# Every second k step of the projections with its two products in reverse order

## The chip, the cores and the metric

The kernel runs on one core of one Trainium2 chip. The metric is the device time of one execution in microseconds (us). PE is the matrix engine, ACT the scalar engine, DVE the vector engine, POOL GpSimd and SP the engine that issues most of the transfers.

## The reference

One layer of a streaming encoder over 256 tokens of width 2048, all in fp32:

```python
u = rms_norm(h, norm_mix[l])
proj = u @ w_in[l]
o_dn = gated_deltanet(...)       # 8 heads, chunked delta rule
o_mla = mla_attention(...)       # 8 heads, latent attention
h = h + jnp.concatenate([o_dn, o_mla], axis=-1) @ w_out[l]
h = h + memory_cross_attention(rms_norm(h, norm_xattn[l]), mem_n, xa_wq, xa_wk, xa_wv, xa_wo)
h = h + conv_ffn(rms_norm(h, norm_ffn[l]), ffn_w_up, ffn_conv, ffn_conv_bias, ffn_w_down)
return rms_norm(h, norm_final)
```

Most of the work is in the weight matrices: 2048 x 4944 in, 2048 x 2048 out, four of 2048 x 2048 in the cross-attention, 2048 x 11264 up and 5632 x 2048 down.

## The kernel before

**A product.** Tokens lie in the free dimension, features on the 128 partitions. A number of 32 bits is kept as the sum of two parts in the fp32r type, high (`wh`, `xh`) and low (`wl`, `xl`), and a product is the sum of three: high by high, high by low, low by high. An input tile for one k chunk of 128 features is 128 x 512: 256 tokens' high parts and beside them their low parts. So `kstep` (lines 112 to 114) needs two matmuls for a k chunk: `wh` by all 512 columns (line 113), then `wl` by the first 256 (line 114). Both add into the same PSUM tile `ps` of 512 columns; its two halves are summed when the tile is evacuated. Each matmul brings a load of its own 128 x 128 block of weights.

**The groups.** A block of 128 output features takes one `ps` and 16 k steps (`gemm_block`), 8 for the two parts of the output projection and 44 for the down projection. The weights come in tiles of 128 x 1024, which are 8 k steps. For each tile SP issues a transfer of 512 KB into `raw`, ACT casts it to `wh` (line 102), DVE subtracts to get `wl` (line 103). `raw`, `wh` and `wl` have four buffers each. While the heads are computed these two run in two pieces of 512 columns.

**Who uses what.** `kstep` runs in the input projection (moving tile `u`), both parts of the output projection (`om`, `od`), the keys' and the output projection of the cross-attention (`mh`, `xo`), the up projection (`fx`) and the down projection (`ga`, `gb`) but its last block. Two other forms stand for comparison. `kstep3` (lines 117 to 119) has three matmuls of 256 columns, all into the first half of `ps`: in the latents' projections (`lath`), in the cross-attention's query projection (`xq`), scores (`kh`) and mixing (`pTx`), and in the last block of the down projection (`ga`, `gb`). The values' projection `v_block` (lines 950 to 952) streams weights past stationary tokens, three matmuls of 512 columns.

**What sets the order.** PE's order is the program's own, written out by hand. While the heads of the two attention groups are worked out, k steps of the input projection and of the output projection's first part are drawn one by one from a queue (`drawn`, `fill`, `until`) wherever PE would wait for the other engines; the constants at lines 20 to 22 say how many. The order on ACT, DVE and POOL is set by a scheduler that works with its own estimate of the durations.

Of the kernel before, what the change touches and what calls it, by code (L numbers as in the profile page):

```python
# [15 lines left out]
PSUM = bass.MemoryType.PSUM  # L16
# k steps drawn from the queue of products where the tensor engine would wait for other engines
F_BEFORE_MLA, F_BEFORE_DN1 = 8, 20                # in blocks
F_MLA, F_LEVEL, F_PRE, F_SOLVE = (6, 2, 4, 9), (3, 4, 5), (21, 6), 45
F_SCAN, F_NORM, F_SQ = 5, 28, 42  # L20

P = 128
T = 256            # tokens, and memory tokens
D = 2048
KC = D // P        # 16 chunks of the model width
DFF = 5632
NF = DFF // P      # 44 chunks of the hidden width
NH = 8             # heads of DeltaNet and of the latent attention
EPS = 1e-6
NEG = -1e30  # L30
B0 = 16            # blocks inverted by substitution, then doubled
LEVELS = (16,)
# a block's entries by column: first and last column, first row
COLS = ((0, 4, 1), (4, 8, 5), (8, 12, 9), (12, 15, 13))
NB = sum((j1 - j0) * (B0 - r0) for j0, j1, r0 in COLS)

# columns of the packed per-partition parameters
_c = 0
# [17 lines left out]

# columns of the constants, which depend on shapes alone
_c = 0
# [12 lines left out]
def trunk(ctx, tc, a):  # L71
    nc = tc.nc
    V, S, PE = nc.vector, nc.scalar, nc.tensor
# [20 lines left out]

# [1 line left out]
    def split_w(raw, n, pieces=1):  # L96
# [13 lines left out]

    # one k step: weights stationary, tokens moving; the two halves of ps are summed later
    def kstep(ps, wh, wl, xh2, first, last):
        PE.matmul(ps[:, 0:512], wh, xh2, start=first, stop=last, skip_group_check=True)  # L113
        PE.matmul(ps[:, 0:256], wl, xh2[:, 0:256], start=False, stop=last, skip_group_check=True)  # L114

# [34 lines left out]

# [1 line left out]
    cg = const.tile([P, NCG], F32, name="cg")  # L152
# [5 lines left out]

    # reciprocal norms as columns, and spread out as rows
    def rstd_col(*accs):  # L160
# [17 lines left out]

    # =================== phase 1: the two head groups ===================
    u = hl_tile("u")  # L180
    ctx.enter_context(tc.manual_schedule(engines={mybir.EngineType.PE}))
    with ExitStack() as ph:
# [11 lines left out]
        with tc.tile_pool(name="xpool", bufs=1) as xpl:  # L194
            xt = xpl.tile([P, KC, T], F32, name="xt")
            nc.sync.dma_start(sm[:, 0:KC], a["sm"][:, 0:KC])
            raw0 = wpool.tile([P, 1024], F32, name="raw", tag="raw")
            for c in range(4):
                nc.sync.dma_start(raw0[:, c * 256:(c + 1) * 256], a["w_in"][0][:, c * 256:(c + 1) * 256])
                nc.sync.dma_start(xt[:, 2 * c:2 * c + 2], a["x"][:, 2 * c:2 * c + 2, :])  # L200
            w0 = [split_w(raw0, 1024, 4)]
            nc.sync.dma_start(xt[:, 8:12], a["x"][:, 8:12, :])
            w0.append(load_w(a["w_in"][1], pieces=2))
            nc.sync.dma_start(xt[:, 12:16], a["x"][:, 12:16, :])
            for k in range(KC):
                split_gain(u(k), xt[:, k], sm[:, C_MIX + k:C_MIX + k + 1])
            ps0 = psg()
            for k in range(KC):
                wh, wl = w0[k // 8]
                j = k % 8  # L210
                kstep(ps0, wh[:, j * P:(j + 1) * P], wl[:, j * P:(j + 1) * P], u(k), k == 0, k == KC - 1)
            ps1 = gemm_block(a["w_in"], 1, u)
            lead = load_w(a["w_in"][4], pieces=2)
            nc.sync.dma_start(cg, a["cg"])
            nc.sync.dma_start(sm[:, KC:NSM], a["sm"][:, KC:NSM])
            nc.sync.dma_start(co, a["co"][:, 0:NCO])
            # sums of squares, half of them on GpSimd
            sqs = [p1.tile([P, 4, T], F32, name="xsq", tag="qkv2", bufs=2) for _ in range(2)]
            for k in range(KC):
                a2 = accs[k % 2]  # L220
                if k < 2:
                    S.activation(a2, xt[:, k], AF.Square)
                else:
                    sq = sqs[k // 4 % 2][:, k % 4]
                    S.activation(sq, xt[:, k], AF.Square)
                    (nc.gpsimd, V)[k % 2].tensor_add(a2, a2, sq)
            nc.sync.dma_start(posi, a["pos"].partition_broadcast(P))

        gbT = p1.tile([P, 2, P], F32, name="gbT")
        # cumulated log decay as columns  # L230
        gc = p1.tile([P, 2, NH], F32, name="gc")
        ngc = p1.tile([P, 2, NH], F32, name="ngc")
        nbe = p1.tile([P, NH], F32, name="nbe")
        # rows of beta and of the cumulated decay, spread over the partitions by way of DRAM
        rows = ph.enter_context(tc.tile_pool(name="rows", bufs=1, space=bass.MemoryType.DRAM))
# [9 lines left out]

# [1 line left out]
        cbuf = [p1.tile([P, T + 3], F32, name=f"cbuf{i}") for i in range(2)]  # L247
# [4 lines left out]

        # a queue of products, drawn on k step by k step where the tensor engine would wait
        queue = []
# [32 lines left out]
        pos, later = [0], []  # L287
        ahead = [2]
# [18 lines left out]
        def dn_qkv(g):  # L307
# [26 lines left out]
            def norms(sq, w, i):  # L334
                ps = psa("c")
                if w == 0:       # squared norms of the queries, as columns
                    for t in range(2):
# [4 lines left out]
                    return  # L342
                # keys of unit length
                n = sq[:, 2 * i:2 * i + 2]
# [9 lines left out]

        # the latents' blocks come first, and the first two are under way
        lats = []
# [6 lines left out]
        with ExitStack() as ms:  # L363
# [3 lines left out]
            nc.sync.dma_start(cm, a["co"][:, K_MLA:K_MLA + 384])  # L367
# [1 line left out]
            ql = mp.tile([P, 4, T], F32, name="ql", tag="kn")  # L369
# [23 lines left out]
            ps = psa()  # L393
# [11 lines left out]

# [1 line left out]
            ang = mp.tile([P, T], F32, name="ang", tag="m1k", bufs=4)  # L407
# [20 lines left out]
            fill(3)  # L428
# [1 line left out]
            kx2 = mp.tile([P, T], F32, name="kx2", tag="m1k", bufs=4)  # L430
# [35 lines left out]
            ps = psa()  # L466
# [5 lines left out]
            ps = psa()  # L472
# [10 lines left out]

# [1 line left out]
            until(Q0 + F_BEFORE_MLA * KC)  # L485

# [1 line left out]
            qpe = mp.tile([P, 4, T], F32, name="qpe")  # L488
# [20 lines left out]

            for i in range(2):           # rotary parts: all first halves, all second halves of 4 heads  # L510
                x1 = mp.tile([P, T], F32, name="qx1", tag="m1k", bufs=4)
# [51 lines left out]
            fill(F[2])  # L563
            for i in range(2):           # 4 heads at a time
                kn = mp.tile([P, 4, T], F32, name="kn", tag="kn")
# [37 lines left out]

# [1 line left out]
        dp = ph.enter_context(tc.tile_pool(name="dn", bufs=1))  # L605
# [10 lines left out]
        def delta(g):  # L616
# [26 lines left out]
            for t in range(2):  # L643
# [3 lines left out]
                V.tensor_mul(dd[t], per4(pm), et[t])  # L647
                # the diagonal blocks, side by side, and each row's turn
                tt[t] = dp.tile([P, 4, P], F32, name="tt", tag="tt", bufs=2)
# [18 lines left out]

            # every partition gets its block, and solves for its column of the block's inverse
            blk = dp.tile([P, 8, NB], F32, name="blk")  # L670
# [43 lines left out]

            # inverse of the unit lower triangular matrix, by doubling its diagonal blocks
            for li in range(len(LEVELS)):
# [20 lines left out]
                fill(F_LEVEL[2])  # L737
            # the last doublings, of which only the blocks under the diagonal are worked out
            for s in (32, 64):
# [33 lines left out]

            # first chunk, before which the state is zero, then the second; the outputs have tokens on partitions
            vn = [None, None]
# [37 lines left out]
            out_sq(po1, 1)  # L813
            # their norm (the query's enters through its epsilon), and back
            V.tensor_add(on, on, nq)
# [52 lines left out]

# [1 line left out]
        mhs = []  # L870
# [30 lines left out]

    # =================== output projection, residual ===================
    x2pool = ctx.enter_context(tc.tile_pool(name="x2pool", bufs=1))
# [158 lines left out]

    # =================== gated convolutional feed-forward ===================
    with ExitStack() as ph:
# [34 lines left out]

        # the square root's table, ahead of its use  # L1100
        warm = small.tile([P, 1], F32, name="warm")
# [26 lines left out]

# [1 line left out]
def _feat(v):  # L1130
# [110 lines left out]
```

## Time and profile before

| | |
|---|---|
| median of 3 runs | 1597.02 us |
| the runs | 1596.87 to 1598.11 us |
| the profiled execution, first to last instruction (its span; the profile lists no other time for it) | 1598.0 us |
| PE busy | 1565.8 us, 98% |
| DVE busy | 1115.5 us, 70% |
| ACT busy | 876.6 us, 55% |
| two lines of `kstep` in the chain that ended last | 71% |

The chain that ended last is the list of work, followed back from the last instruction, in which each piece was waited for by the next. PE's busy time counts a product from its start to its modelled end, and these overlap: with products one behind another PE is always busy, whatever the distance between their starts. So its pace is read from the starts in the timeline, or from the mean duration of a group, and not from the busy share.

### The profile page before, as it was taken

How to read it: one execution, taken by the hardware profiler on the slowest of the kernel's cores; microseconds unless marked ns; L12 is line 12 of the kernel's file. 1: busy time of each engine (PE TensorE's matmuls, PEld its weight loads, DVE VectorE, ACT ScalarE, POOL GpSimd, SP SyncE). 2: the span in 40 equal slices, each digit the busy share in tenths (PEclk: the TensorE clock that was granted, in tenths of full speed). 3: DMA queues.
4: the chain of work that ended last, by engine and by line, in shares of the span. 5: the costliest groups of instructions: out<-in, count | busy, mean ns of one | idle time of the engine just before them, and what ended most of it. 6: DMA issues, size and time to landing. Idle time of an engine off the chain costs nothing.

```text
span 1598.0 us, 24744 instructions
## 1 busy us (share of the span) xinstructions
PE 1565.8 (98%) x9386; PEld 1367.6 (86%) x9386; DVE 1115.5 (70%) x1810; ACT 876.6 (55%) x1474; POOL 145.2 (9%) x152
## 2 busy tenths in 40 slices
PE   7999999999999999999999999999999999999996
PEld 5887887888888889999888888888888888888886
DVE  7787688687975555666777777777787876445453
ACT  7767666847654444454556555555555555433341
POOL 2224011002310000000110000000000000111112
PEclk9999999999999999999999999999999999999998
DMA  7564444353655555544555555555555556665663
GB/s 251 173 204 143 144 134 136 126 199 120 215 194 186 188 190 189 178 137 146 179 189 180 188 188 184 185 185 186 187 188 189 186 184 178 185 191 177 194 182 107
DMA packets 80775, 282.25 MB, mean 177 GB/s; under 512 B 9392, under 2 KB 10304, under 8 KB 80656
## 3 DMA queue, kind: packets, MB, share of 16 engines
q1 hardware_dynamic: 79344, 277.86, 53.5%
q0 software_dynamic: 1312, 2.80, 0.6%
q8 instruction: 74, 1.21, 0.3%
q14 instruction: 45, 0.37, 0.1%
HBM read 277.83 MB, written 2.11 MB: 175 GB/s over the span
## 4 chain that ended last, share of the span: by engine, by line
PE 89%; DVE 6%; ACT 3%; issue 1%; DMA 1%; SPq 0%; DVEq 0%; ACTq 0%
PE psg L113 47%; PE psg L114 24%; PE psg L117 3%; PE psg L118 2%; PE psg L119 2%; DVE wl L103 2%; PE psg L952 2%; PE psg L950 2%; PE psg L951 2%; ACT wh L102 1%; DVE qkv L322 1%; DMA raw<-in_w_out_dram 1%; PE psa L612 0%; PE psa L531 0%; PE psa L530 0%
## 5 line engine op out<-in xcount | busy, mean ns | idle before, releaser
L103 DVE TENSOR_TENSOR wl<-raw,wh 128x1024 fp32r<-128x1024 f32 (+2 forms) x614 | 648.7, 1062 | 388.2 <-ACT wh L102 385.1
L102 ACT CAST wh<-raw 128x1024 fp32r<-128x1024 f32 (+2 forms) x614 | 551.5, 908 | 598.9 <-PE psg L113 373.7
L113 PE MATMUL psg<-fx,wh 128*128 128x512 f32 x1408 | 497.8, 397 | 0.0
L114 PE MATMUL psg<-fx,wl 128*128 128x256 f32 x1408 | 395.6, 281 | 0.0
L113 PEld LDWEIGHTS psg<-fx,wh 128*128 128x128 f32 x1408 | 264.7, 188 | 65.3
L114 PEld LDWEIGHTS psg<-fx,wl 128*128 128x128 f32 x1408 | 264.3, 188 | 0.0
L113 PE MATMUL psg<-u,wh 128*128 128x512 f32 x624 | 233.9, 413 | 9.0 <-DVE u L141 8.0
L114 PE MATMUL psg<-u,wl 128*128 128x256 f32 x624 | 177.5, 284 | 1.7 <-DVE wl L103 1.7
L113 PEld LDWEIGHTS psg<-u,wh 128*128 128x128 f32 x624 | 119.5, 191 | 39.6 <-DVE u L141 8.9
L113 PE MATMUL psg<-gb,wh 128*128 128x512 f32 x420 | 149.1, 397 | 0.0
L114 PEld LDWEIGHTS psg<-u,wl 128*128 128x128 f32 x624 | 119.6, 192 | 3.4 <-DVE wl L103 2.7
L114 PE MATMUL psg<-gb,wl 128*128 128x256 f32 x420 | 118.0, 281 | 0.0
L113 PEld LDWEIGHTS psg<-gb,wh 128*128 128x128 f32 x420 | 79.0, 188 | 19.5
L113 PE MATMUL psg<-mh,wh 128*128 128x512 f32 x256 | 90.7, 398 | 0.0
L113 PE MATMUL psg<-xo,wh 128*128 128x512 f32 x256 | 90.7, 398 | 0.0
L1081 DVE SCALAR_TENSOR_TENSOR y<-ub,sm,y 128x256 f32<-128x256 f32 x176 | 84.8, 482 | 3.1
L113 PE MATMUL psg<-ga,wh 128*128 128x512 f32 x240 | 85.5, 397 | 0.0
L114 PEld LDWEIGHTS psg<-gb,wl 128*128 128x128 f32 x420 | 78.8, 188 | 0.0
L114 PE MATMUL psg<-xo,wl 128*128 128x256 f32 x256 | 71.9, 281 | 0.0
L114 PE MATMUL psg<-mh,wl 128*128 128x256 f32 x256 | 71.9, 281 | 0.0
L117 PE MATMUL psg<-xq,wh 128*128 128x256 f32 x256 | 71.2, 278 | 0.0
L118 PE MATMUL psg<-xq,wh 128*128 128x256 f32 x256 | 70.9, 277 | 0.0
(405 smaller groups left out, 2487.2 us busy)
## 6 DMA issues: line engine op xcount, KB each, us to landing
raw<-in_w_up_dram SPq DMA_DIRECT2D x176, 512.0 KB, 3.5
raw<-in_w_down_dram SPq DMA_DIRECT2D x80, 512.0 KB, 4.1
raw<-in_w_in_dram SPq DMA_DIRECT2D x77, 512.0 KB, 3.8
raw<-in_w_out_dram SPq DMA_DIRECT2D x32, 512.0 KB, 3.6
raw<-in_xa_wk_dram SPq DMA_DIRECT2D x32, 512.0 KB, 3.5
raw<-in_xa_wv_dram SPq DMA_DIRECT2D x32, 512.0 KB, 3.5
raw<-in_xa_wq_dram SPq DMA_DIRECT2D x32, 512.0 KB, 3.5
raw<-in_xa_wo_dram SPq DMA_DIRECT2D x32, 512.0 KB, 3.5
```

The source lines that it names most:

```text
L102: S.copy(wh[:, c], raw[:, c])
L103: V.tensor_sub(wl[:, c], raw[:, c], wh[:, c].bitcast(F32))
L113: PE.matmul(ps[:, 0:512], wh, xh2, start=first, stop=last, skip_group_check=True)
L114: PE.matmul(ps[:, 0:256], wl, xh2[:, 0:256], start=False, stop=last, skip_group_check=True)
L117: PE.matmul(ps[:, 0:T], wh, xh2[:, 0:T], start=first, stop=False)
L118: PE.matmul(ps[:, 0:T], wh, xh2[:, T:2 * T], start=False, stop=False)
L119: PE.matmul(ps[:, 0:T], wl, xh2[:, 0:T], start=False, stop=last)
L322: V.scalar_tensor_tensor(t[:, i], cb[:, j:j + T], sm[:, ch + j:ch + j + 1], t[:, i], ALU.mult, ALU.add)
L950: PE.matmul(pss[t], xh, wh[:, wk], start=(k == 0), stop=False)
L951: PE.matmul(pss[t], xh, wl[:, wk], start=False, stop=False)
L952: PE.matmul(pss[t], xl, wh[:, wk], start=False, stop=(k == KC - 1))
L1081: V.scalar_tensor_tensor(y, b[:, j:j + T], sm[:, cw + j:cw + j + 1], y, ALU.mult, ALU.add)
```

## The change

`kstep` gets a flag that turns with every step. On the first step of a group the order is as before, high then low. On the next it is low, then high, and so on in turn. A group always begins with the high part, which clears `ps`. Groups, and the tiles of 8 steps and pieces of 4 in them, have an even number of steps, so it is always the odd step of a tile that is reversed. Nothing else changes in the program; comments are gone, which moves the line numbers: lines 113 and 114 of before are 122 and 120 of after, 102 and 103 stay, 132 becomes 140.

```diff
     def kstep(ps, wh, wl, xh2, first, last):
-        PE.matmul(ps[:, 0:512], wh, xh2, start=first, stop=last, skip_group_check=True)
-        PE.matmul(ps[:, 0:256], wl, xh2[:, 0:256], start=False, stop=last, skip_group_check=True)
+        rev = turn_[0] and not first
+        turn_[0] = not rev
+        for lo in ((True, False) if rev else (False, True)):
+            if lo:
+                PE.matmul(ps[:, 0:256], wl, xh2[:, 0:256], start=False, stop=last, skip_group_check=True)
+            else:
+                PE.matmul(ps[:, 0:512], wh, xh2, start=first, stop=last, skip_group_check=True)
```

On PE, the first tile of weights of the up projection before (`fx0` is the input's first half, numbers are buffers):

```order
L113 MATMUL psg_8569<-fx0_8477,wh_8572 128x512
L114 MATMUL psg_8569<-fx0_8477,wl_8573 128x256
L113 MATMUL psg_8569<-fx0_8477,wh_8572 128x512
L114 MATMUL psg_8569<-fx0_8477,wl_8573 128x256
L113 MATMUL psg_8569<-fx0_8477,wh_8572 128x512
L114 MATMUL psg_8569<-fx0_8477,wl_8573 128x256
```

and after:

```order
L122 MATMUL psg_8569<-fx0_8477,wh_8572 128x512
L120 MATMUL psg_8569<-fx0_8477,wl_8573 128x256 x2
L122 MATMUL psg_8569<-fx0_8477,wh_8572 128x512 x2
L120 MATMUL psg_8569<-fx0_8477,wl_8573 128x256 x2
L122 MATMUL psg_8569<-fx0_8477,wh_8572 128x512 x2
```

The products of one size now stand in twos; the number of each is the same.

On ACT, in the input projection near 50 us, where casts for the next k steps stand between the evacuations of finished blocks (`half`), before:

```order
L102 CAST wh_506<-raw_504 128x512 x2
L424 ACTIVATE cos_735<-ang_733 128x256
L425 ACTIVATE cos_735<-cos_735 128x256
L102 CAST wh_531<-raw_529 128x512
L132 COPY half_499<-psg_458 128x256
L102 CAST wh_531<-raw_529 128x512
L145 ACTIVATE kacc_304<-cl_300 128x256
```

and after:

```order
L102 CAST wh_506<-raw_504 128x512 x2
L432 ACTIVATE cos_735<-ang_733 128x256
L433 ACTIVATE cos_735<-cos_735 128x256
L140 COPY half_499<-psg_458 128x256
L102 CAST wh_531<-raw_529 128x512 x2
L153 ACTIVATE kacc_304<-cl_300 128x256
```

The evacuation has moved ahead of one cast of half a tile. The scheduler moved others in the same way, mostly before 470 us; SP's order is unchanged.

## Rows read from the trace of the kernel before

**Rows 1.** The page: span, busy time of PE, chain by line.

```profile
span 1598.0 us, 24744 instructions
PE 1565.8 (98%) x9386; PEld 1367.6 (86%) x9386; DVE 1115.5 (70%) x1810; ACT 876.6 (55%) x1474; POOL 145.2 (9%) x152
PE psg L113 47%; PE psg L114 24%; PE psg L117 3%; PE psg L118 2%; PE psg L119 2%; DVE wl L103 2%; PE psg L952 2%; PE psg L950 2%; PE psg L951 2%; ACT wh L102 1%; DVE qkv L322 1%; DMA raw<-in_w_out_dram 1%; PE psa L612 0%; PE psa L531 0%; PE psa L530 0%
```

**Rows 2.** Waits of PE: total us, times, longest.

```profile
PE psg L113 <- DVE u L141: 8.0, 3, 6.5
...
PE psg L114 <- DVE wl L103: 1.7, 3, 1.2
...
PE psg L113 <- ACT wh L102: 0.9, 1, 0.9
```

**Rows 3.** Timeline of PE, up projection: start us, length us, product.

```profile
1000.20 0.40 PE L113 MATMUL psg<-fx,wh 128*128 128x512 f32 x1
1000.44 0.28 PE L114 MATMUL psg<-fx,wl 128*128 128x256 f32 x1
1000.56 0.40 PE L113 MATMUL psg<-fx,wh 128*128 128x512 f32 x1
...
1001.26 0.40 PE L113 MATMUL psg<-fx,wh 128*128 128x512 f32 x1
```

**Rows 4.** Products by form, count, busy us, mean ns: up, query, values, down, mixing.

```profile
L113 PE MATMUL psg<-fx,wh 128*128 128x512 f32 x1408 | 497.8, 397 | 0.0
L114 PE MATMUL psg<-fx,wl 128*128 128x256 f32 x1408 | 395.6, 281 | 0.0
...
L117 PE MATMUL psg<-xq,wh 128*128 128x256 f32 x256 | 71.2, 278 | 0.0
...
L119 PE MATMUL psg<-xq,wl 128*128 128x256 f32 x256 | 70.9, 277 | 0.0
...
L952 PE MATMUL psg<-wh,mh 128*128 128x512 f32 x128 | 50.3, 393 | 0.0
L950 PE MATMUL psg<-wh,mh 128*128 128x512 f32 x128 | 50.2, 392 | 0.0
L951 PE MATMUL psg<-wl,mh 128*128 128x512 f32 x128 | 49.9, 390 | 0.0
...
L118 PE MATMUL psb<-pTx,vh 128*128 128x256 f32 x16 | 4.5, 283 | 0.0
...
L118 PE MATMUL psg<-ga,wh 128*128 128x256 f32 x16 | 4.5, 281 | 0.0
```

**Rows 5.** Timeline of PE, query projection, three products a step.

```profile
619.20 0.28 PE L117 MATMUL psg<-xq,wh 128*128 128x256 f32 x1
...
619.54 0.28 PE L117 MATMUL psg<-xq,wh 128*128 128x256 f32 x1
```

**Rows 6.** Timeline of PE, mixing in the cross-attention, three products a step.

```profile
709.02 0.28 PE L117 MATMUL psb<-pTx,vh 128*128 128x256 f32 x1
...
709.38 0.28 PE L117 MATMUL psb<-pTx,vh 128*128 128x256 f32 x1
```

**Rows 7.** Line 113 in two stretches: us, PE busy (count), clock, DMA.

```profile
0.00:407.00 407.00, 281.00 (x752) 0.99 0.50 164
407.00:1598.00 1191.00, 957.63 (x2708) 1.00 0.56 181
```

**Rows 8.** ACT's longest wait, then subtraction and cast by form.

```profile
ACT wh L102 <- PE psg L113: 373.7, 270, 3.5
...
L103 DVE TENSOR_TENSOR wl<-raw,wh 128x1024 fp32r<-128x1024 f32 x412 | 506.9, 1230 | 326.1 <-ACT wh L102 323.5
...
L102 ACT CAST wh<-raw 128x1024 fp32r<-128x1024 f32 x412 | 433.1, 1051 | 528.8 <-PE psg L113 350.0 <-issue 94.7 <-PE psg L952 50.8
```

**Rows 9.** Timeline of PE, input projection just behind a gap.

```profile
321.38 0.39 PE L113 MATMUL psg<-u,wh 128*128 128x512 f32 x1
...
322.07 0.39 PE L113 MATMUL psg<-u,wh 128*128 128x512 f32 x1
...
322.77 0.40 PE L113 MATMUL psg<-u,wh 128*128 128x512 f32 x1
```

More of the change, by code (lines that the diff above doesn't have):

```diff
@@ L109, in load_w @@
         return split_w(raw, n, pieces)
+    turn_ = [False]
     def kstep(ps, wh, wl, xh2, first, last):
-        PE.matmul(ps[:, 0:512], wh, xh2, start=first, stop=last, skip_group_check=True)
-        PE.matmul(ps[:, 0:256], wl, xh2[:, 0:256], start=False, stop=last, skip_group_check=True)
+        rev = turn_[0] and not first
[5 more added lines that the diff above has]
+                PE.matmul(ps[:, 0:512], wh, xh2, start=first, stop=last, skip_group_check=True)
     def kstep3(ps, wh, wl, xh2, first, last):
```

## The prediction

> **What bounds the kernel now.** I read the page first. The matrix engine is busy for 1565.8 of 1598.0 us, and of the chain that ended last 71% is the two lines that the change touches [rows 1]. Then the waits of PE: the longest group is 8.0 us, and waits for the weights (wl, wh) come to 2.6 us [rows 2]. So the time is not a wait that could be removed. It is the pace at which PE puts one product behind another, and the third view is of that pace.
>
> I call H a product of 512 columns (high part) and L one of 256 (low part). In the feed-forward stretch H starts at 1000.20, L at 1000.44, the next H at 1000.56 and, two k steps later, another at 1001.26 [rows 3]: 1.06 us for three k steps of 768 columns, 0.353 each, some 0.235 from H to L and 0.118 from L to H. Each product brings one weight load with it, before the change and after it. The table by form has means to the nanosecond: 397 for H and 281 for L [rows 4]; their sum of 678 is 325 more than the k step's 353, so a mean is about 162 more than the step to the next product. The difference of two such means is therefore a difference of pace.
>
> The same columns run at other paces elsewhere in this trace. The query projection of the cross-attention has only L products, three for a step of 768 columns: from 619.20 to 619.54, 0.340 a step [rows 5], with means of 278 and 277 [rows 4]. The last block of the down projection has the same three products at 281, and the mixing with the values needs 709.02 to 709.38, 0.360 a step [rows 4, 6]. The values' projection has only H products, and their means are 393, 390 and 392, not 397 [rows 4]. So a product's pace depends on its neighbours or on the phase in which it meets them, by several per cent, with no wait shown. That is what this change can move.
>
> **The change part by part.** There are 752 k steps before 407 us and 2708 after it, 3460 in all [rows 7], which is 1730 pairs. First step of a pair: H L as before. Second step: L H. Nothing is added: matmuls, loads, columns and transfers stay as many, and the high part still opens each group. The pattern H L H L becomes H L L H: of the four steps from product to product, two (H to L, L to H) stay, and the other H to L and L to H become one L to L and one H to H.
>
> H term. In the values' projection an H between two H takes (393 + 390 + 392) / 3 = 391.7, against 397: 5.3 ns less [rows 4]. In the new order each H has one H and one L neighbour, so I count half, 2.65, twice a pair: 5.3 ns. The bounds are 0 and all of it, 10.6.
>
> L term. An L between two L takes 277 to 278 in the query projection, 281 in the last block of the down projection, 283 in the mixing, against 281: from 3.7 less to 2 more [rows 4]. Half of it, twice a pair, is between 3.7 less and 2 more. The last block comes straight out of the H L pattern, and there L is no faster than in it; the query projection has far more products (256 for each of its three lines). I take the middle of those two, 1.9 less.
>
> That is 7.2 ns a pair. After 407 us PE hardly waits: (2708 / 2) x 7.2 = 9.7 us. Before 407 us the steps fill gaps between the small products of the heads, in short runs, and less filling makes some waits longer; I count half: 376 x 3.6 = 1.4 us. Together 11 us. The profiled span is 1598.0, which is 1.0 above the median of the runs and within their spread, so I take the sum off the median: 1597 - 11 = 1586.
>
> What is moved besides:
> - The high part of a weight tile is now read last, not last but one, so its buffer comes free one L later, 0.118 us, and the cast that refills it (ACT line 102, which waits for PE's line 113 in 270 cases, 373.7 us in sum [rows 8]) starts that much later. Behind it in ACT's order stand evacuations of finished products. Four buffers rotate, so the cast still runs about three tiles of 8 x 0.353 = 2.8 us ahead of its use; cast and subtraction need 1.05 and 1.23 us [rows 8]. Cost: none. Without that cover it would be 0.118 us a tile, some 430 tiles, 51 us. The low part's buffer comes free earlier, and the weight transfers on SP, whose order doesn't change, wait for the subtraction and so move by 0.12 us at most.
> - An odd step is never the first of a tile or of a cast piece, so no product asks for the low part before it did.
> - At the end of a block H now comes last and evacuation waits for it. Both products had to be done before, so this costs nothing beyond the pace.
> - The order of work on ACT, DVE and GpSimd shifts a little, mostly before 470 us: evacuations stand one cast earlier. A cast then waits for a block's end and one copy more. PE waited only 0.9 us for casts and 1.7 us for subtractions in the whole run [rows 2], and tiles are two ahead there. I count 0, with 3 us to either side.
>
> One rule speaks against any effect. The rows show 0.235 and 0.118 us for products of 512 and 256 columns, and other paces for the same columns [rows 3 to 6]. The Trainium skill (TensorE: Matmul & The Clock Gate, Step-by-step: what each phase is for) says that the engine reads the streamed operand and the weights through two independent ports, and that loading the next weights takes no read bandwidth from the running product. By that rule the order can't matter and the sum would be 0, which is the first rival below; the trace has not agreed with it so far, as the same L product stands at 277, 281 and 283 ns.
>
> **The rivals.**
> *No change.* Each load costs its product the same in this stream whatever stands next to it. For it: the two means hold over 1408 products each [rows 4], and behind a gap two steps take 0.69 (321.38 to 322.07) but the next two 0.70 again (322.07 to 322.77) [rows 9]. The stream is drawn to its slow pace, and the last block stayed in it with L products alone. Against it: H products run faster among themselves [rows 4]. Time: 1597, within 3.
>
> *The fast pace.* The new pattern settles where the query projection is, 0.340 a step [rows 5]. Then 3460 x 13.3 ns = 46 us, 1551; for half of that, 1574. For it: this pace exists with as many loads per product, and the means of 256 products of a line are near it [rows 4]. Against it: it is there with L products alone.
>
> *Slower: the pairs of short products.* Two L in a row must each have a weight load beside only 0.118 us of streaming, and before the change an H always followed. If L to L then runs as in the mixing, 0.120 [rows 6], and H gains nothing, a pair costs 2 x 1.7 = 3.3 ns more: 5.8 us, 1603. If all products go at that pace, 0.360 against 0.353 a step, it is 23 us, 1620. It decides from an L to L step over 0.118 plus what H to H gives back.
>
> **How the numbers follow.** Forecast, some of the interference goes, 4 to 20 us: 0.43. No change: 0.30. Fast pace, over 20 us: 0.14. Slower: 0.13. About 0.2%, 3 us, is what a measurement of this kernel can tell from no change. So faster 0.57, same 0.30, slower 0.13. The range reaches down to three quarters of the fast pace (1597 - 35 = 1562) and up to the short pairs' 1603; about 0.85 lies in it.
>
> **What would show it.** In the profile of the changed kernel the mean of the 512-column groups (fx, gb, ga) should be near 394 instead of 397 and that of the 256-column groups near 280. From the first H of a pair to the next pair's first H the timeline should show 0.70 us where it is 0.707 now. PE's waits should stay under 25 us. If the means stay at 397 and 281, the first rival holds; 388 and 276 are the fast pace; an L over 282 is the slow rival. A longer wait of PE for wl or wh would show that the cover of the casts was thinner than I think, and then the whole sum is wrong.

## The result, and the profile after

The changed kernel takes 1580.49 us (median of 4, 1578.94 to 1581.17), the kernel before in the same session 1596.94. The ratio is 0.989, with an interval of 0.9878 to 0.9902: 16.4 us faster, where 11 were forecast, inside the range of 1562 to 1603.

The profiled execution took 1580.7 us in all, 1.8 more than its span. If as much lies around the span of before, that execution of before was one of the slower ones (1599.8), and so the two spans differ by 19.1 us, more than the medians do.

The page of the changed kernel, to be read beside [rows 1]: span and busy time.

```profile
span 1578.9 us, 24577 instructions
PE 1546.1 (98%) x9386; PEld 1358.5 (86%) x9386; DVE 1119.3 (71%) x1810; ACT 889.3 (56%) x1473; POOL 147.9 (9%) x152
```

The matrix engine has as many products as before, 9386, and as large a share of the span. Its waits, as total us, times, longest:

```profile
PE psg L122 <- DVE u L149: 8.2, 3, 6.5
...
PE psg L120 <- DVE wl L103: 1.7, 3, 1.1
...
PE psg L122 <- ACT wh L102: 0.6, 1, 0.6
```

Against [rows 2] nothing has gone: 8.0 is 8.2, 1.7 is 1.7, 0.9 is 0.6. So the time was not taken from a wait. The timeline of PE in the up projection (a line may merge two products of one form; start, us) shows where it was taken:

```profile
1000.31 0.39 PE L120 MATMUL psg<-fx,wl 128*128 128x256 f32 x2
1000.54 0.62 PE L122 MATMUL psg<-fx,wh 128*128 128x512 f32 x2
1001.00 0.39 PE L120 MATMUL psg<-fx,wl 128*128 128x256 f32 x2
1001.23 0.62 PE L122 MATMUL psg<-fx,wh 128*128 128x512 f32 x2
```

From one pair of high products to the next, 1000.54 to 1001.23, two k steps take 0.69 us, where [rows 3] have 0.707. The table by form gives it to the nanosecond (count, busy us, mean ns):

```profile
L122 PE MATMUL psg<-fx,wh 128*128 128x512 f32 x1408 | 439.8, 393 | 0.0
L120 PE MATMUL psg<-fx,wl 128*128 128x256 f32 x1408 | 277.6, 279 | 0.0
...
L122 PE MATMUL psg<-gb,wh 128*128 128x512 f32 x420 | 133.4, 393 | 0.0
L120 PE MATMUL psg<-gb,wl 128*128 128x256 f32 x420 | 82.8, 278 | 0.0
```

Against 397 and 281 in [rows 4], the high product is 4 ns shorter and the low one 2 to 3: four products, some 13 ns a pair. The two stretches of [rows 7] say the same. The table of windows for line 122, with as many k steps in each stretch as before:

```profile
0.00:405.50 405.50, 249.43 (x752) 0.99 0.50 164
405.50:1578.90 1173.40, 846.50 (x2708) 1.00 0.57 184
```

The stretch behind the heads went from 1191.0 to 1173.4 us: 17.6 us for 1354 pairs, 13.0 ns each. The stretch of the heads went from 407.0 to 405.5: 1.5 us for 376 pairs. The windows are cut at half microseconds; by the last product of the first output projection, which starts at 406.8 us before and at 405.0 after, the two parts are 17.3 and 1.8 us.

### The profile page after: what moved, and what is told of

Read it like the earlier page. It is cut to its first block, busy times and chain, and to the rows that moved or that the text cites. A ratio compares the mean times of both kernels' runs of the same rounds, so it can differ in the third digit from the quotient of the medians.

```text
span 1578.9 us, 24577 instructions
## 1 busy us (share of the span) xinstructions
PE 1546.1 (98%) x9386; PEld 1358.5 (86%) x9386; DVE 1119.3 (71%) x1810; ACT 889.3 (56%) x1473; POOL 147.9 (9%) x152
## 4 chain that ended last, share of the span: by engine, by line
PE 88%; DVE 5%; ACT 4%; issue 1%; DMA 1%; SPq 0%; DVEq 0%; ACTq 0%
PE psg L122 46%; PE psg L120 23%; PE psg L125 3%; PE psg L126 3%; PE psg L127 3%; PE psg L960 2%; PE psg L959 2%; PE psg L958 2%; DVE wl L103 2%; ACT wh L102 1%; DMA raw<-in_w_out_dram 1%; PE psa L620 0%; PE psa L539 0%; DVE qkv L330 0%; DVE hT L1132 0%
## 5 line engine op out<-in xcount | busy, mean ns | idle before, releaser
L102 ACT CAST wh<-raw 128x1024 fp32r<-128x1024 f32 (+2 forms) x614 | 550.8, 909 | 401.5 <-PE psg L122 243.2
L122 PE MATMUL psg<-fx,wh 128*128 128x512 f32 x1408 | 439.8, 393 | 0.0
L120 PE MATMUL psg<-fx,wl 128*128 128x256 f32 x1408 | 277.6, 279 | 0.0
L122 PE MATMUL psg<-u,wh 128*128 128x512 f32 x624 | 207.7, 404 | 8.9 <-DVE u L149 8.2
L122 PEld LDWEIGHTS psg<-fx,wh 128*128 128x128 f32 x1408 | 212.0, 188 | 0.0
L140 ACT COPY half<-psg 128x256 f32<-128x256 f32 x143 | 53.2, 372 | 154.9 <-PE psg L122 154.7
L120 PE MATMUL psg<-u,wl 128*128 128x256 f32 x624 | 134.3, 289 | 1.7 <-DVE wl L103 1.7
L122 PEld LDWEIGHTS psg<-u,wh 128*128 128x128 f32 x624 | 99.3, 191 | 12.5 <-DVE u L149 9.0
L120 PE MATMUL psg<-gb,wl 128*128 128x256 f32 x420 | 82.8, 278 | 0.0
L141 DVE TENSOR_TENSOR ub<-psg,half 128x256 f32<-128x256 f32 x88 | 37.4, 425 | 60.1 <-ACT half L140 60.1
L127 PE MATMUL psg<-xq,wl 128*128 128x256 f32 x256 | 70.9, 277 | 0.0
```

Of the source, the lines that this page charges most:

```text
L102: S.copy(wh[:, c], raw[:, c])
L127: PE.matmul(ps[:, 0:T], wl, xh2[:, 0:T], start=False, stop=last)
L140: S.copy(t, ps[:, T:2 * T])
L141: V.tensor_add(out, ps[:, 0:T], t)
```

## The experiments

Two questions stood. Where does the gain arise, and what in the order of the products makes it? As before, H is a product of 512 columns and L one of 256.

### Only the later or only the early part

The first kernel has the change only from the second part of the output projection on, the second only ahead of it (there the flag starts as True and is set to False at the same place).

```diff
-        PE.matmul(ps[:, 0:512], wh, xh2, ...)
+        rev = turn_[0] and not first and on_[0]
+        turn_[0] = not rev
+        if not rev:
+            PE.matmul(ps[:, 0:512], wh, xh2, ...)
         PE.matmul(ps[:, 0:256], wl, xh2[:, 0:256], ...)
+        if rev:
+            PE.matmul(ps[:, 0:512], wh, xh2, ...)
...
         mhs.append(hl_half("mh1", x2pool))
+        on_[0] = True
```

> The change only behind the heads' stretch (from the second part of the output projection on); before it the order of before. By the two profiles this part of the change brings 17.3 of 19.1 us: 1580 to 1582 us. If the order of the other engines, which the change shifts in the heads' stretch, costs what is missing there (3 us), this kernel is no slower than the changed one, 1579 to 1580 us.

> The change only in the heads' stretch, the order of before behind it. By the two profiles it brings 1.8 us, 1595 us; at 13.3 ns for each of 376 pairs it would be 5 us, 1592 us; if the shifted order of the other engines takes it back altogether, 1597 us.

Measured: the late part alone 1580.62 us against 1597.42, ratio 0.9892 (0.9876 to 0.9907), which is the whole gain within the interval. The early part alone 1595.99, ratio 0.999 (0.9981 to 0.9999): 1.4 us. So the stretch of the heads holds little of it. The kernel with the late part alone leaves out most of the shifted order of the other engines and is as fast as the changed one, so that order is not where the gain comes from. Whether it costs something in the heads' stretch, which a gain in pace there makes up for, these two runs don't tell.

The first of these kernels has the two places of H on lines of their own, and its table by form tells them apart (line 118 is the H that stands ahead of its L, line 121 the one behind):

```profile
L118 PE MATMUL psg<-fx,wh 128*128 128x512 f32 x704 | 280.4, 398 | 0.0
L119 PE MATMUL psg<-fx,wl 128*128 128x256 f32 x1408 | 277.6, 279 | 0.0
L121 PE MATMUL psg<-fx,wh 128*128 128x512 f32 x704 | 273.2, 388 | 0.0
```

The saving is not spread over the products. The H that follows an H and goes ahead of an L is as slow as any before (398), the H that follows two L is 10 ns shorter (388).

### Low part first in every step

Theory A, formed from the profile after: each step from H to L costs 13.3 ns and the rest is free, and the change halves the number of such steps.

```diff
-        PE.matmul(ps[:, 0:512], wh, xh2, ...)
-        PE.matmul(ps[:, 0:256], wl, xh2[:, 0:256], ...)
...
+        for f in ((hi, lo) if first else (lo, hi)):
+            f()
```

> Low part first in every k step but a group's first, so the stream is L H L H: as many steps from a 512-column product to a 256-column one as before the change. Theory A (each step from 512 to 256 columns costs 13.3 ns, as the profile after has it: 236 + 118 against 226 + 113; all other steps are free): as before, about 1594 to 1597 us, a k step 0.353 us. Rival B (the gain comes from the high part standing last or first in a step, or from the other engines' order): 1580 us. Rival C (a pace is set by the average of a product's neighbours): as before, 1597 us.

Measured: 1594.72 us, ratio 0.9979 (0.997 to 0.9988). Standing last in a step does H no good while H and L alternate. The run is 3.5 us below before, and each group does begin with two low products in a row. B is out. A fits; C, which had it as before, is a little off, and the runs of eight below decide on it.

### Products of one size alone

Two kernels take the change of size away. In the first, H is made two products of 256 columns with a load each. As it is written, a group is opened twice and its sum is not the whole one; the products, their columns and their loads are those of a full sum. In the second, L is made 512 columns long.

```diff
-        PE.matmul(ps[:, 0:512], wh, xh2, start=first, ...)
+        PE.matmul(ps[:, 0:256], wh, xh2[:, 0:256], start=first, ...)
+        PE.matmul(ps[:, 256:512], wh, xh2[:, 256:512], start=first, ...)
```

> The high part's product of 512 columns is made two of 256, each with its own weight load; all products have 256 columns. Theory A: no step from 512 to 256 is left, so a k step takes 0.340 us everywhere and the whole about 1597 - 46 = 1551 us, up to 1556 with what the stretch of the heads gives back. Rival D (the stream locks into the slow pace in which it starts, whatever the sizes; the last block of the down projection had 0.353 with just these products): 0.353 us a k step, 1597 us. A third load a step, were it to cost as in the mixing (0.360), would give 1620 us.

```diff
-        PE.matmul(ps[:, 0:256], wl, xh2[:, 0:256], start=False, ...)
+        PE.matmul(ps[:, 0:512], wl, xh2, start=False, ...)
```

> The low part's product is taken over all 512 columns too, which adds low part by low part to the second half of the sum (work that the kernel before leaves out). All products have 512 columns, the weights still change between wh and wl. Theory A: 2 x 226.7 = 453 ns a k step, 100 more than before: 1597 + 346 = 1943 us. Rival E (the price is on the change from wh to wl in the loads, not on the size): 467 ns a step, 1989 us. If products of 512 run as in the values' projection, 229 each: 458 ns, 1960 us.

Measured: 1596.81 us (0.9991, 0.9981 to 1.0) and 1983.19 us (1.241, 1.2391 to 1.2428). Theory A falls twice: it wanted 1551 and 1943. The tables by form, the split kernel first:

```profile
L113 PE MATMUL psg<-fx,wh 128*128 128x256 f32 x1408 | 395.7, 281 | 0.0
L114 PE MATMUL psg<-fx,wh 128*128 128x256 f32 x1408 | 395.6, 281 | 0.0
L115 PE MATMUL psg<-fx,wl 128*128 128x256 f32 x1408 | 395.6, 281 | 0.0
```

and with 512 columns for both:

```profile
L113 PE MATMUL psg<-fx,wh 128*128 128x512 f32 x1408 | 560.5, 398 | 0.0
L114 PE MATMUL psg<-fx,wl 128*128 128x512 f32 x1408 | 553.4, 393 | 0.0
```

Without any change of size all products are still slow: 281 for every one of 256 columns, 398 and 393 for those of 512. In the same execution of the split kernel the query projection of the cross-attention, the same three products, keeps the means of [rows 4], 278 and 277:

```profile
L118 PE MATMUL psg<-xq,wh 128*128 128x256 f32 x256 | 71.2, 278 | 0.0
```

So the sizes alone don't set the pace. The second kernel came near rival E's 1989, but the next run has H after H with `wh` alone at 395, as slow as the 398 and 393 here, so E's reason is not the cause either.

### Long runs of one kind

Behind the heads, a tile's eight H stand together, then its eight L, and the next tile of the group in reverse.

```diff
+    def ktile(ps, wh, wl, x, n, first, last):
...
+        for lo in ((True, False) if rev else (False, True)):
+            for j in range(n):
+                w = (wl if lo else wh)[:, j * P:(j + 1) * P]
+                c = 256 if lo else 512
+                PE.matmul(ps[:, 0:c], w, x(j)[:, 0:c], ...)
```

> The change's order in the heads' stretch; behind it, the eight high products of a weight tile stand together, then the eight low ones, and in reverse in the next tile of a group. Behind 407 us this leaves about 181 steps from 512 to 256 columns where the changed kernel has 1354. Theory A: 1173 x 13.3 ns = 15.6 us less than the changed kernel, about 1565 us. Rival D (long runs of one size fall into the slow phases seen in the trace of before, 229 ns for a product of 512 in the values' projection, 118 for one of 256 in the last block of the down projection): 2708 x (2.3 + 4.7) = 19 us given back, 1580 to 1584 us. Rival C (half of the difference between a product among its own kind and one in alternation): about 5 us less than the changed kernel, 1575 us.

Measured: 1579.47 us, ratio 0.9882 (0.9868 to 0.9897), no different from the changed kernel. Theory A (1565) is out, and so is C (1575). The table by form tells why:

```profile
L130 PE MATMUL psg<-fx,wh 128*128 128x512 f32 x1408 | 343.0, 395 | 0.0
L130 PE MATMUL psg<-fx,wl 128*128 128x256 f32 x1408 | 174.5, 276 | 0.0
```

The runs of L are clean, 276, but those of H are not, 395. Against the changed kernel's 279 and 393, L is 3 shorter and H 2 longer, and the step of 768 columns is where the change had it. Rival D's total (1580 to 1584) is close, but it had both runs slow, and the L are not. The starts in this trace show more than the means: from the first H of a run, behind the L, to the next it is 226 ns, and from then on 236 and 231 in turn, all with `wh`.

Theory F, formed from these four: the pace hangs on the products that went before. An L right behind an H is slow, the next L clean, an H behind a clean L clean, an H behind an H slow. The last part holds on the mean only, as the alternation of 236 and 231 shows.

### The same sizes over other columns

Two k steps at a time, H H L L. The sizes follow each other as in the change, but neighbours no longer stream the same columns.

```diff
+        held_.append((ps, wh, wl, xh2, first, last))
+        if len(held_) < 2:
+            return
...
+        for ps, wh, wl, xh2, first, last in two:
+            PE.matmul(ps[:, 0:512], wh, xh2, ...)
+        for ps, wh, wl, xh2, first, last in two:
+            PE.matmul(ps[:, 0:256], wl, xh2[:, 0:256], ...)
```

> Two k steps at a time: both high products, then both low ones (H H L L H H L L). The sizes follow each other as in the changed kernel, but no product streams the same columns as the one before it. Theory F (the pace hangs on the sizes that went before: a low product right behind a high one takes 118, the next low one 113, a high one behind that 226, a high one behind a high one 236): 693 ns for two steps as in the changed kernel, 1580 us, within 3. Rival G (what counts is that a low and a high product over the same columns stand together): the gain is gone, 1597 us.

Measured: 1587.27 us, ratio 0.9928 (0.9914 to 0.9943). The total missed both, the pace is F's:

```profile
L121 PE MATMUL psg<-fx,wh 128*128 128x512 f32 x1408 | 439.4, 393 | 0.0
L123 PE MATMUL psg<-fx,wl 128*128 128x256 f32 x1408 | 277.6, 279 | 0.0
```

393 and 279 are the means of the changed kernel. What the total lacks was lost in the heads' stretch: there the last product of the first output projection starts at 413.4 us, in the changed kernel at 405.0, and PE's idle time in that stretch is 26.1 us where it is 19.8. That holding a step back until the next one comes leaves gaps unfilled is the likely reason. G is out: shared columns are not what counts.

### Some products split, and runs of a third kind

If an L behind an L is clean, then splitting some H into two products of 256 columns should pay.

```diff
+        if n_[0] % 2 == 0:
...
+        else:
+            PE.matmul(ps[:, 0:256], wl, xh2[:, 0:256], ...)
+            PE.matmul(ps[:, 256:512], wh, xh2[:, 256:512], ...)
+            PE.matmul(ps[:, 0:256], wh, xh2[:, 0:256], ...)
```

> Pair order, and in every odd step the high product of 512 columns is made two of 256, with a load each: H L, then L L L. Theory F (behind a low product that itself follows a low one, everything runs clean): 226 + 118.3 + 3 x 113.3 = 684 ns for two steps where the changed kernel has 693 and the kernel before 707: 39 us less than before, 1562 us with 4 us lost in the heads' stretch. Rival D (products of 256 lock into 117.7 as in the run with the high product split everywhere): 235 + 4 x 118 = 706, 1597 us.

The second kernel of this kind splits three steps of four (`% 4`).

> As the run before, with three of four steps split: H L, then nine products of 256. Theory F: 226 + 118.3 + 9 x 113.3 = 1364 ns for four steps, 341 a step against 353: 43 us less than before, 1558 us with 4 us lost in the heads' stretch. Rival D: 353 a step, 1597 us. If the third load of a step has a price of its own, as the mixing suggests (120 a product): 1610 us.

In the third kernel of this kind a tile is worked off in runs of eight with one part of the weights and one half of the columns.

```diff
+        runs = [(wh, 0, j) for j in range(n)] + [(wh, 256, j) for j in range(n)] + [(wl, 0, j) for j in range(n)]
...
+        for w, c, j in runs:
+            PE.matmul(ps[:, c:c + 256], w[:, j * P:(j + 1) * P], x(j)[:, c:c + 256], ...)
```

> The change's order in the heads' stretch; behind it, a weight tile is worked off in three runs of 256 columns: the high part by the first half of the columns, the high part by the second half, the low part by the first half (a group opens with one product of 512). Theory J (a run over the same half of the columns with one weight part runs clean, as the runs of low products did with 113.3 ns): 340 to 341 ns a step behind 407 us, 2708 x 6 ns = 16 us less than the changed kernel, 1564 us. Rival D (only products of 256 lock into 117.5, as in the two runs with split steps): 353 to 355 ns, 1597 to 1603 us.

Measured: 1602.26 us (1.0025, 1.0015 to 1.0036), 1604.11 us (1.0035, 1.0023 to 1.0046) and 1597.30 us (0.9991, 0.9982 to 1.0). F and J are wrong in all three by 33 to 46 us. Every second step split, by form:

```profile
L117 PE MATMUL psg<-fx,wh 128*128 128x512 f32 x704 | 280.3, 398 | 0.0
L118 PE MATMUL psg<-fx,wl 128*128 128x256 f32 x704 | 197.8, 281 | 0.0
...
L120 PE MATMUL psg<-fx,wl 128*128 128x256 f32 x704 | 197.1, 280 | 0.0
```

and the runs of eight:

```profile
L129 PE MATMUL psg<-fx,wh 128*128 128x256 f32 x2640 | 339.7, 281 | 0.5 <-DVE fx L160 0.5
L129 PE MATMUL psg<-fx,wl 128*128 128x256 f32 x1408 | 194.3, 281 | 0.0
```

An L behind an L (line 120) stays at 280, an H behind L's (line 117) at 398, and in the last kernel even the run of eight low products is at 281, where the same run stood at 276 between runs of H. So F is no rule for a product and its predecessor; it describes the patterns with whole H that were measured. By the starts, the second L behind an H goes to the next product after 113 ns in the changed kernel and in the runs of eight, and after 118 ns in the kernel with every second step split (line 120), with the same H and L ahead of it. A stream of 256 columns can be in either pace, and what decides it lies further back or ahead than that; these runs don't show which. That such a stream stays in its slow pace, as the forecast's first rival had it, is what all the split kernels show.

### Half a load

The last pair asks whether the loss comes through the weight load that runs beside a product. In all steps but a group's first the weights are 64 columns wide, once in the order of before (the edit shown) and once in the order of the change. The edit halves two things: the columns of a load, and the rows of `ps` that a product writes (`ps[0:m]`).

```diff
+        m = P if first else 64
-        PE.matmul(ps[:, 0:512], wh, xh2, ...)
-        PE.matmul(ps[:, 0:256], wl, xh2[:, 0:256], ...)
+        PE.matmul(ps[0:m, 0:512], wh[:, 0:m], xh2, ...)
+        PE.matmul(ps[0:m, 0:256], wl[:, 0:m], xh2[:, 0:256], ...)
```

> The order of before, but in every step but a group's first the weights are 64 columns wide, not 128, for both products (half of each output block is left out). The streamed columns stay as they were; each load is half as long. Theory H (what makes 235 + 118 of 226.7 + 113.3 is the load that runs beside a product): half of the 13.3 ns a step goes or more, 340 to 347 ns, 1551 to 1575 us. Rival I (the streamed columns or the writing of the sums make it, the loads don't matter): 353 ns, 1597 us.

> The change's order and weights of 64 columns in every step but a group's first (half of each output block is left out). Beside the run with the order of before and such weights (1578 us). Theory H (the change gains by what the loads cost, and half a load costs half): the change gains about half as much, 6.7 ns for a pair and not 13.3: some 8 to 9 us less, 1569 to 1571 us. Rival K (loads and order have nothing to do with each other): the change gains its 16 to 17 us here too, 1562 us.

Measured: 1578.22 us (0.9874, 0.9859 to 0.9889) with the old order and 1576.65 us (0.986, 0.9844 to 0.9877) with the new one. Products and loads of the old order, by form:

```profile
L114 PE MATMUL psg<-fx,wh 128*64 128x512 f32 x1320 | 461.6, 390 | 0.0
L115 PE MATMUL psg<-fx,wl 128*64 128x256 f32 x1320 | 369.6, 280 | 0.0
```

```profile
L115 PEld LDWEIGHTS psg<-fx,wl 128*64 128x64 f32 x1320 | 176.9, 134 | 0.0
```

and the products of the new one:

```profile
L122 PE MATMUL psg<-fx,wh 128*64 128x512 f32 x1320 | 416.9, 392 | 0.0
L120 PE MATMUL psg<-fx,wl 128*64 128x256 f32 x1320 | 268.2, 279 | 0.0
```

The streamed columns are those of before, and the load is shorter, 134 ns where the whole one takes 188 (the changed kernel's line for it stands below), which is not half as long, as the expectation had it. H falls from 397 to 390, L stays at 280 where it was 281, and in the old order the timeline has three steps in 1.04 us:

```profile
1099.63 0.39 PE L114 MATMUL psg<-fx,wh 128*64 128x512 f32 x1
...
1100.67 0.39 PE L114 MATMUL psg<-fx,wh 128*128 128x512 f32 x1
```

That is 347 ns a step, where it was 353 before and is 340 at the fast pace, and 20 us of the 46 that the fast pace was to bring. So half of the excess of 13 ns a step went with this edit, as theory H had it, and the streamed columns alone, one half of rival I, don't make the loss. The other half of I, the writing of the sums, is not out: half as many rows are written, and no run here halves the load and not the rows. With half loads the new order brings 1.6 us by the medians, within the two intervals, not 16 as K had it, and not 8 to 9 as theory H had it, so the size of that expectation was wrong. The order and the narrow weights seem to be two handles on the same loss: each brings the step to 347, and together they hardly go below it. The whole load of the changed kernel:

```profile
L122 PEld LDWEIGHTS psg<-fx,wh 128*128 128x128 f32 x1408 | 212.0, 188 | 0.0
```

This is where a rule can be weighed. The rows say that weights of half the width leave H up to 7 ns shorter. The Trainium skill (TensorE: Matmul & The Clock Gate, Step-by-step: what each phase is for) has it that the two streams read through ports of their own and that loading the next weights takes no read bandwidth from the running product. If a load cost nothing in any other way either, the pace could not move with it; here the pace moved when load and written rows were halved together, so these runs neither bear the rule out nor refute it. As the forecast read it, that the order can't matter, it failed: the order gave 16.4 us. The same page (LDWEIGHTS (loading the stationary operand)) gives a load's time in ns as its columns by 1.2: an estimate of 53 ns less for 64 columns less, with which 188 - 134 = 54 agrees. The whole length doesn't: by that formula 128 columns are an estimated 107 ns, and the row has 188.

## Why the prediction was right, and where it was not

**The bound.** Right. PE's pace was the time; its waits stayed as they were, and the busy counts too.

**The H term.** It was mis-sized. I took the H of the values' projection (391.7) for a clean one and gave half of the difference to each H, 5.3 ns a pair. The means of 393 against 397 make it some 8 ns a pair, and the late kernel shows how they come about, 398 and 388: one H of the pair gets nothing, the other 9 to 10. Half each, for having one H as a neighbour, was the wrong picture: an H in an unbroken run of H with `wh` is at 395, so an H beside an H is hardly the gain, and the H that gains stands behind two L. The direction was right for a reason that the runs don't bear out, and that is partly luck.

**The L term.** It was mis-sized as well, 1.9 ns a pair where the means went from 281 to 279 or 278, 4 to 6 ns a pair. The row of the last block, which stays at 281 among L's, was given half the weight, but there the low product stands among split products. The split kernels show that such streams stay slow by themselves, and the runs of L between runs of H are clean (276). The query projection's row was the one to go by.

**The sum behind 407 us.** Forecast 9.7 us, measured 17.6 by the spans, 13.0 ns a pair instead of 7.2. The late kernel has 16.8 by its times. Both terms were too small, so the whole came out at 16.4 us and not at 11.

**The stretch of the heads.** Forecast at half the price, 1.4 us. Measured 1.5 by the spans and 1.4 by the early kernel. At the measured 13.0 ns a pair half would have been 2.4: a smaller share was kept than I thought, and that the number came out is luck, a price too low by a share too high. Longer waits, the reason given, don't show, as far as idle time can show between products that overlap: PE's idle time in that stretch is 19.5 us before (407.0 - 387.55) and 19.8 after (405.5 - 385.69):

```profile
0.00:407.00 407.00, 387.55 (x2442) 0.99 0.50 164
```

```profile
0.00:405.50 405.50, 385.69 (x2442) 0.99 0.50 164
```

The means gained less there. In the input projection H falls from 413 to 404, but L rises from 284 to 289, 4 ns a step where it is 6 in the up projection; why, these rows don't tell. Before and after:

```profile
L113 PE MATMUL psg<-u,wh 128*128 128x512 f32 x624 | 233.9, 413 | 9.0 <-DVE u L141 8.0 <-ACT wh L102 0.9
L114 PE MATMUL psg<-u,wl 128*128 128x256 f32 x624 | 177.5, 284 | 1.7 <-DVE wl L103 1.7
```

```profile
L122 PE MATMUL psg<-u,wh 128*128 128x512 f32 x624 | 207.7, 404 | 8.9 <-DVE u L149 8.2 <-ACT wh L102 0.6
L120 PE MATMUL psg<-u,wl 128*128 128x256 f32 x624 | 134.3, 289 | 1.7 <-DVE wl L103 1.7
```

**What hides the rest.** Right. The cast that starts one L later was covered, and waits for wl and wh were 2.3 us where they had been 2.6. Much of ACT's waiting now stands at another line. In the changed kernel, two lines of ACT's waits:

```profile
ACT wh L102 <- PE psg L122: 243.2, 206, 2.5
ACT half L140 <- PE psg L122: 154.7, 117, 3.4
```

The cast's wait of [rows 8] fell from 373.7 to 243.2 us, and 154.7 now stand ahead of an evacuation, where 0.9 stood before; the scheduler has put the evacuation ahead of the cast. PE did not wait longer for either.

**The rivals.** No change: wrong, though its reason, a stream that is drawn to its slow pace, is what the four split kernels met. The slow rival: two L in a row don't cost more; the pair goes from 281 to 279. Its price also took both L of a pair for slow (2 x 1.7), though only one of them has an L behind it; with one it is 2.9 us, 1600. The fast pace of 0.340 was not reached for a whole k step by the change or in any experiment.

**What stays open.** Why the H H L L pattern settles at 347 ns a step, neither at 340 nor at 353, and why split streams lock at 353. That half-width weights take away half of the loss is shown; whether it is the load beside a product or the rows that it writes, and which product meets it in which phase, is not. No run that does the whole work beat the changed kernel by more than its interval.

## What to carry to other kernels

When an engine is busy all the time and nothing waits, compare the step from one start to the next for the same form in different stretches of one trace: a difference of a few per cent there is a loss that the busy share can't show. Where products of two lengths alternate, try the order in which like stands beside like; it is an edit of a few lines, and here it gave 1%. Don't build further on the pattern without a measurement: four more kernels that a simple rule called better than this one (the runs of eight, and the three under "Some products split") gained nothing on it.

## What was not expected of the hardware

- The same product of 256 columns has a mean of 276 to 278 or of 281 ns in one execution (278 and 281 in the kernel with every H split), with no wait in the trace and at the same granted clock (1.00 behind the heads). The streams of split products in the projections stayed at the slow one, 280 to 281.
- Weights of half the width, with a load of 134 ns and not 188 and half the rows written, make the stream faster: 347 ns for 768 columns against 353, all of it on H (390 against 397; L 280 against 281).
- Products of 512 columns in an unbroken run are not at their best (395 with one part of the weights, 398 and 393 with both in turn), and one directly behind two of 256 is (388).
